# Two gate pieces of mixer B moved into the first 24 blocks of the attention of a hybrid attention layer

## The chip, the cores and the metric

The kernel runs on one core of a Trainium2 chip. The metric is the device time of one execution in microseconds (us). A core has a matrix engine (TensorE, PE in the profile; its weight loads are listed apart as PEld), a vector engine (VectorE, DVE), a scalar engine (ScalarE, ACT), a general engine (GpSimd, POOL), and SyncE (SP), which here only issues DMAs. Each engine works through its own instructions strictly in the order in which the program lists them.

## The reference

One transformer layer works on 128 context tokens ("prompt") and 1024 latent tokens. Cut to what matters here:

```
h = rmsnorm(x, norm_gain) * (1 + scale) + shift
q_a, k_a, v_a, g_a, q_b, k_b, v_b, g_b = split(h @ w_in)
o_a = attention of mixer A (all latent keys and the cached context)
o_b = attention of mixer B (a window of 128, the cached context, a sink)
x + gate * (concat(o_a * silu(g_a), o_b * silu(g_b)) @ w_out)
```

Each mixer has 8 query heads of 64 columns, in 2 groups that share keys and values. The change concerns `g_b`, 512 columns that are computed for all 1152 tokens, and the point at which `w_out` is brought into its working form.

## The kernel before, in words

One pass of PE is not precise enough here, so each 32-bit operand is kept as a high part and a low part, and a product takes three matmuls, high by high, high by low, low by high. `silu(g)` is stored in DRAM (`g_dram`) and read back per unit.

The stages before the attention: the normalised tokens `h` are made and kept in SBUF, high and low, in three thirds of 512, 256 and 384 tokens; then come the gates of A, the queries of A and B, keys and values, and the gates of B. `gates` (L305) walks over thirds and over `ch`, four pieces of 128 columns: one piece is 24 matmuls, 8 steps over k with three products each. That gives 12 pieces for mixer B, the last four 384 tokens wide. Between the matmuls of the last 8 pieces the kernel also runs 24 "max" items and two closings (`beside`, L1050): a score product `pmx` on PE (L881) and its row maximum on DVE (L882), for units 0 and 2.

In the same pieces `w_out` is prepared. It has 16 slabs of 128 by 512. `load_wo` fetches a slab, and `split_wo` (L1032 on) makes its high part with a DVE cast (L1037) and its low part with a subtraction (L1038), on POOL for odd slabs and on DVE for even ones. The parts lie where `h` lay, once that is read for the last time. `WO_STEPS` lists the slabs that are split beside the gates (0 to 10) and `WO_LATE` those split in the attention (11 to 15), each with a block number for its load; its split follows three blocks later.

The attention is a list of units, in the order token tile `t`, group `g`, mixer `m`, the prompt last: 36 units, 0 to 35. A unit of mixer A has nine blocks of keys, one of mixer B three or four. One loop (L1256 on) goes over all blocks, and a "tick" of an agenda starts each. Block `s` issues, in this order: what the agenda holds for this tick, the scores of block `s` (two matmuls `st` into one of two PSUM banks "B", then ACT's exp L1123 and cast L1127, and the low part on POOL L1131; for mixer B four transposes `st` L1115 and a cast L1116), loads of `w_out`, the items that are due (max items for a later unit of A; for a unit of B two matmuls `sn`, a DVE custom operation L942 and ACT's exp L928), up to 2.5 matmuls of the output projection (`po`, L1212) if some are ready, and last the value products of block `s - 3` (`pv`, L1141 to L1144).

A unit of A needs the negated row maxima as extra rows of its query tile: `finish` reduces them, two ticks later PE transposes them (`ptm`, L900), and DVE writes them into `qb` (L901), which the second `st` matmul (L1121) reads. The tick of `finish` is set by `MX_END`: ten blocks after the start of the unit two before.

When the last block of a unit is through, four steps follow at ticks given by `END_AT`: `inverse` (ACT, L1153 or L1155 and L1156), `gated` (two DVE products L1165 that read `pv`, one on POOL), `parts` (high and low output parts `ogh`, `ogl`), and, for a unit of B, the release of 24 output matmuls. `pv` has two banks, so `pv` of a unit waits for `gated` of the unit two before. Output matmuls left at the end run after the loop.

Of the kernel before, what the change touches and what calls it, by code (L numbers as in the profile page):

```python
# [34 lines left out]
KS = (0, 1, 4, 5, 2, 3, 6, 7)  # L35
PL_DVE = (4,)
LAG = 3
LEAD = 4
EARLY = (0, 2)
LOADED = 4  # L40

# [3 lines left out]
MX_AT = (-4, -3, -2, -2, -1, 4, 5, 5, 7, 7, 8, 8)  # L45
MX_FIRST = (0, 1, 2, 2, 3, 4, 4, 5, 6, 6, 7, 8)
PH_DVE = 0
MX_END = 10
SPLIT_LAG = 2

WO_LATE = {12: 8, 13: 9, 11: 21, 14: 22, 15: 23}

WO_STEPS = ((0, 4, 4), (1, 5, 5), (2, 6), (3, 7), (4, 8, 6), (5, 9), (6, 11), (7, 12, 10), (8, 13), (9, 14), (10, 16))
TURN = 2
PUT_LOW = 2
QUERY_AT = (0, 2, 3, 6)
# [52 lines left out]
def hybrid_step(ctx, tc, x_prompt, x_sample, cache_k_a, cache_v_a, cache_k_b, cache_v_b,  # L109
# [800 lines left out]
    def weight_items(i):  # L910
# [93 lines left out]


    wo_raw, wo_parts, wo_big = {}, {}, {}
    STAGE = {0: (1, 0, 7), 1: (0, 0, 7), 2: (1, 0, 6), 3: (0, 0, 6), 4: (1, 0, 7), 5: (0, 0, 7), 6: (1, 0, 7),
             7: (0, 1, 6), 8: (1, 1, 6), 9: (1, 1, 4), 10: (0, 1, 6)}

    def h_slot(lo, i, c, name):  # L1010

# [62 lines left out]
    spare = h_slot(1, 2, 4, "spare").bitcast(F32)  # L1074
    wo_big[2] = h_slot(1, 2, 0, "wo_big2")
    gate = spare[:, 0:512], wo_big[2].bitcast(F32)[:, 1024:1536]
    for n in range(2):
        nc.sync.dma_start(gate[n], gate_row[0:1, 512 * n : 512 * n + 512].to_broadcast([P, 512]))
# [55 lines left out]
    def values(i, b, last, blk, ph, pl):  # L1134
        t, m, g = units[i]
        _, vh, vl = blk
        if b == 0:
            pvb[i] = bank("C", f"pv{i}")
        pv = pvb[i]
        two = vh.rearrange("p s d -> p (s d)")  # L1140
        nc.tensor.matmul(pv, two, ph, start=(b == 0), stop=False)  # L1141
        if m == 0:
            nc.tensor.matmul(pv[0:64, :], vl, ph, start=False, stop=False)  # L1143
        nc.tensor.matmul(pv, two, pl, start=False, stop=last)  # L1144
# [12 lines left out]

        def gated():
            rs = v["rs"]
            o = 768 + 256 * (i % 3)  # L1160
            of = spare[:, o : o + 256].rearrange("p (c n) -> p c n", c=2)
            pvv = pv[0:64, :].rearrange("p (c s n) -> p c s n", s=2, n=P)
            srv = rs.rearrange("p (c s n) -> p c s n", s=2, n=P)
            for s in range(2):
                nc.vector.tensor_tensor(of[64 * s : 64 * s + 64], pvv[:, :, s, :], srv[:, :, s, :],  # L1165
                                        op=ALU.add if m else ALU.mult)
# [32 lines left out]
    def out_items(t, g):  # L1199
# [3 lines left out]
        def mm(n, k, p):  # L1203
# [12 lines left out]
            if k == KS[-1] and p == 2:  # L1216
# [4 lines left out]

        ks = KS[4 * g : 4 * g + 4]
        return [lambda n=n, k=k, p=p: mm(n, k, p)
                for kk in ((ks[:2], ks[2:]) if last else (ks,)) for n in range(2) for k in kk for p in range(3)]

    slots, start = [], []
    for i in range(NU):
# [10 lines left out]
    for i, (t, m, g) in enumerate(units):  # L1238
        if i in EARLY:
            continue  # L1240
        if m == 0:
            items, done = max_items(i)
            at, end = [start[i - 2] + a for a in (MX_AT if i > 2 else MX_FIRST)], start[i - 2] + MX_END
            if t == 0:
                end = start[i] - LEAD
                at = [end - 1]
# [9 lines left out]
            put(s, f)  # L1256
        put(end, done)

    credit, live = 0.0, []
    load_gate(0)  # L1260
    load_gate(1)
    for s in range(len(slots) + LAG + PROMPT_END[3]):
# [83 lines left out]
```

## Time and profile before

| what | value |
| --- | --- |
| median of 3 runs | 711.83 us (711.57 to 713.92) |
| the profiled execution's own time | 711.52 us |
| its span, first to last instruction | 709.6 us |
| PE busy | 691.6 us, 97% |
| DVE, ACT, POOL busy | 469.3, 409.9, 334.2 us |
| last 8 gate pieces of B with max items | 270.5 to 303.1 us |
| blocks 0 to 11 of the attention (units 0 and 1) | 303.18 to 321.90 us |
| blocks 12 to 23 (units 2 and 3) | 321.90 to 341.64 us |
| block 24 | 341.64 to 344.69 us |

A row of the timeline gives the start of an instruction from the span's start, how long it took, engine, line and operation, what it writes and reads, and in brackets the idle time of its engine before it and what ended that. PE's matmuls overlap: a 384-column matmul is listed with 0.34 us, but the next can begin about half of that later, so PE's real pace is the distance between two starts, and PE counts as busy while a gap is shorter than the tail of the matmul before it.

### The profile page before, as it was taken

The page shows a single profiled execution, that of the slowest core. Times are in us where ns is not written, and L with a number is a line of the kernel's source. Part 1 is how long each engine was busy: PE and PEld are TensorE (multiplying, and loading weights), DVE is VectorE, ACT ScalarE, POOL GpSimd, SP SyncE. Part 2 cuts the span into 40 slices and gives each one's busy share as a digit, 9 for nine tenths or more (in the row PEclk, how much of TensorE's full clock was granted, in tenths as well). Part 3 has the DMA queues.
Part 4 walks back from the last instruction along what each step waited for, and adds up shares of the span by engine and source line. Part 5 has one row for each costly group of instructions (what it writes and reads, how often), then busy time and mean ns, then how long its engine had stood idle before and what let it go on. Part 6 is the DMA issues. An engine that isn't in the chain of part 4 may idle for free. (4 is left out here: it accounts for less than half of the span.)

```text
span 709.6 us, 10604 instructions
## 1 busy us (share of the span) xinstructions
PE 691.6 (97%) x3508; PEld 558.5 (79%) x3508; DVE 469.3 (66%) x1019; ACT 409.9 (58%) x829; POOL 334.2 (47%) x356
## 2 busy tenths in 40 slices
PE   7999999999999999989999999999999999999987
PEld 4778988878787889966788888888888888787865
DVE  4667257967848945647867578666775776675662
ACT  5646412412403431188777887787778777877760
POOL 3547023233213421256756655665576557555660
PEclk9999999999999999999999999999999999999999
DMA  8962283358353116332222121212221221222323
GB/s 316 415 211 102 78 302 74 90 154 263 84 139 104 37 39 215 123 108 57 78 68 85 50 82 53 71 57 75 68 82 38 79 71 50 78 72 70 104 67 121
DMA packets 53560, 78.58 MB, mean 111 GB/s; under 512 B 7096, under 2 KB 25720, under 8 KB 52608
## 3 DMA queue, kind: packets, MB, share of 16 engines
q1 hardware_dynamic: 45328, 65.96, 28.1%
q10 hardware_dynamic: 8176, 11.94, 6.3%
q8 instruction: 28, 0.46, 0.3%
q14 instruction: 28, 0.23, 0.1%
HBM read 58.69 MB, written 19.18 MB: 110 GB/s over the span
## 5 line engine op out<-in xcount | busy, mean ns | idle before, releaser
L1131 POOL TENSOR_TENSOR pl<-pe,ph 128x512 fp32r<-128x512 f32 x130 | 167.7, 1292 | 145.0 <-DVE nm L942 67.5
L882 DVE TENSOR_REDUCE mx<-pmx 128x1 f32<-128x384 f32 x192 | 101.4, 552 | 56.3 <-PE pmx L881 54.8
L1123 ACT ACTIVATE pe<-st 128x512 f32<-128x512 f32 x146 | 86.8, 594 | 28.2 <-PE st L1121 27.4
L1127 ACT CAST ph<-pe 128x512 fp32r<-128x512 f32 x146 | 90.6, 621 | 4.8
L1141 PE MATMUL pv<-ph,v_hi 128*128 128x512 f32 x208 | 82.8, 398 | 2.2 <-DVE spare L1165 2.2
L1144 PE MATMUL pv<-pl,v_hi 128*128 128x512 f32 x208 | 82.4, 396 | 0.0
L1212 PE MATMUL po<-wo,ogh 128*128 128x512 f32 x216 | 72.6, 395 | 0.2 <-DVE yt L1219 0.2
L174 POOL TENSOR_TENSOR rs_q<-ms_q,mhalf 128x8 f32<-128x8 f32 x18 | 34.1, 1896 | 80.9 <-DVE ms_q L172 80.9
L942 DVE CUSTOM_DVE_ANT_0 sn<-sn,mask,nsink 128x512 f32<-128x512 f32 (+1 forms) x64 | 46.4, 724 | 38.0 <-PE sn L939 37.6
L881 PE MATMUL pmx<-kha,qt 128*128 128x384 f32 x192 | 61.2, 363 | 0.4 <-ACT pen L928 0.2
L1120 PE MATMUL st<-qt,kha 128*128 128x512 f32 x144 | 58.2, 404 | 1.9 <-ACT pe L1123 1.1
L1121 PE MATMUL st<-qb,kla 68*128 68x512 f32 x144 | 57.5, 399 | 1.1 <-DVE qb L901 1.1
L1143 PE MATMUL pv<-ph,v_lo 128*64 128x512 f32 x146 | 57.6, 395 | 0.0
L1144 PEld LDWEIGHTS pv<-pl,v_hi 128*128 128x128 f32 x208 | 39.2, 189 | 16.4
L928 ACT ACTIVATE pen<-sn,nm 128x512 f32<-128x512 f32 (+2 forms) x72 | 45.0, 626 | 6.5 <-DVE nm L942 3.1
L1116 ACT CAST ph<-st 128x512 fp32r<-128x512 f32 x62 | 36.4, 587 | 19.9 <-PE st L1115 18.7
L1141 PEld LDWEIGHTS pv<-ph,v_hi 128*128 128x128 f32 x208 | 39.3, 189 | 10.6 <-ACT ogh L1177 2.4
L646 ACT CAST qo0q<-ptq 128x512 fp32r<-128x512 f32 x18 | 10.6, 586 | 60.7 <-PE ptq L643 55.8
L1212 PEld LDWEIGHTS po<-wo,ogh 128*128 128x128 f32 x216 | 40.0, 188 | 6.8 <-DVE yt L1219 0.6
L1117 DVE TENSOR_TENSOR pl<-st,ph 128x512 fp32r<-128x512 f32 x62 | 42.5, 686 | 2.7 <-ACT ph L1116 2.1
L1212 PE MATMUL po<-wo,ogl 128*128 128x512 f32 x108 | 42.6, 394 | 0.0
L881 PEld LDWEIGHTS pmx<-kha,qt 128*128 128x128 f32 x192 | 35.6, 191 | 6.4 <-DVE mx L882 1.3
(213 smaller groups left out, 1699.2 us busy)
## 6 DMA issues: line engine op xcount, KB each, us to landing
qt<-qd SPq DMA_DIRECT2D x36, 256.0 KB, 3.0
wm<-in_w_mod_ss_dram SPq DMA_DIRECT2D x7, 1024.0 KB, 10.0
qd<-qo0q ACTq DMA_DIRECT2D x36, 128.0 KB, 2.4
qd<-qo1q ACTq DMA_DIRECT2D x36, 128.0 KB, 2.4
sgl<-gd SPq DMA_DIRECT2D x36, 128.0 KB, 2.2
out_dram<-yt SPq DMA_DIRECT2D x17, 256.0 KB, 2.0
xn<-in_x_sample_dram SPq DMA_DIRECT2D x8, 512.0 KB, 7.2
wg<-in_w_mod_g_dram SPq DMA_DIRECT2D x4, 1024.0 KB, 8.3
```

What stands on the lines that cost most here:

```text
L881: nc.tensor.matmul(pm[:, 0:384], lhs, kha[:, g, 3 * b : 3 * b + 3, :], start=True, stop=True)
L882: nc.vector.tensor_reduce(mx[:, h, b : b + 1], pm[:, 0:384], axis=AX.X, op=ALU.max)
L942: nc.vector.tensor_tensor_reduce(s, s, mask[:, m0 : m0 + n], -1.0, nsink[:, 4 * g + h : 4 * g + h + 1], op0=ALU.add, op1=ALU.min, accum_ou ...
L1120: nc.tensor.matmul(s, kh, qtile[i], start=True, stop=False)
L1121: nc.tensor.matmul(s, kl, qbtile[i], start=False, stop=True)
L1123: nc.scalar.activation(pe, s, AF.Exp)
L1127: nc.scalar.copy(ph, pe)
L1131: nc.gpsimd.tensor_tensor(pl, pe, ph, op=ALU.subtract)
L1141: nc.tensor.matmul(pv, two, ph, start=(b == 0), stop=False)
L1143: nc.tensor.matmul(pv[0:64, :], vl, ph, start=False, stop=False)
L1144: nc.tensor.matmul(pv, two, pl, start=False, stop=last)
L1212: nc.tensor.matmul(po[n], a, wo_parts[KT * n + k][lo], start=(k == KS[0] and p == 0), stop=(k == KS[-1] and p == 2))
```

## The change

The last two pieces of B's gates (`ch` 2 and 3, the third of 384 tokens) are no longer computed in the gate stage: `gb` runs six pieces after the first four instead of eight, and the max items stand closer (over 48 steps of k and not 64). ACT copies the 256 columns of weights that the two pieces need, high and low, into the places of `h`'s second third (`keep`, 16 copies); these are the places in which slabs 8 to 11 of `w_out` are later put. The 48 matmuls (`late_product`) go into a queue of which each block takes two (`LATE_RATE`), just ahead of its value products; they fill PSUM banks "D" and "E", which the output projection takes over afterwards. `silu` of a finished piece is then built from ACT's Exp and three DVE operations on 384 columns, add, reciprocal and product, since the attention's function table on ACT holds no Silu. The result tile is one of the three buffers `pe` of the attention's exponentials. Slabs 7, 8, 9 and 10 of `w_out` are split in the attention and no longer beside the gates, and 11 to 15 later than before.

Three smaller edits: the maxima of a unit of A are closed three blocks before the unit starts (`MX_LEAD`; for a unit behind a three-block unit of B, which are units 4 and 30, this is one block earlier than before, for the others the same), with `LEAD` one larger for the prompt's units; units 31 and on of the latent tokens (that is, unit 31) take their last steps at ticks 1, 2, 3, 5 and not 1, 4, 6, 9 (`END_LAST`); and the prompt's first 24 output matmuls run one half of the columns after the other.

The diff, cut to its core:

```diff
-LEAD = 4
+LEAD = 5
...
-MX_END = 10
+MX_LEAD = 3
...
-WO_LATE = {12: 8, 13: 9, 11: 21, 14: 22, 15: 23}
+WO_LATE = {8: 22, 9: 23, 12: 25, 13: 26, 7: 28, 10: 29, 11: 32, 14: 33, 15: 35}
...
+LATE_RATE = 2
...
+END_LAST = (1, 2, 3, 5)
+ENDING = 31
...
-    beside[:2] = 0.0, (len(beside[2]) + 0.5) / 64
+    beside[:2] = 0.0, (len(beside[2]) + 0.5) / 48
...
-    for n, _ in enumerate(gb):
-        if n == 4:
-            for i in (7, 8, 9):
-                load_wo(i)
+    kept = {}
+    def keep(k):
+        for lo, src in enumerate((W_GB.hi[k], W_GB.lo[k])):
+            if k % 2 == 0:
+                kept[lo, k // 2] = h_slot(lo, 1, k, f"kept{lo}_{k}")
+            o = 256 * (k % 2)
+            nc.scalar.copy(kept[lo, k // 2][:, o : o + 256], src[:, 256:512])
+    for n in range(6):
+        next(gb)
+        if n == 3:
+            for k in range(KT):
+                later(1 + k // 2, lambda k=k: keep(k))
...
+    def late_product(ch, w, x, k, first, last):
+        if first:
+            pgl[ch] = bank("DE"[ch % 2], f"pgl{ch}")[:, 0:384]
+        o = 256 * (k % 2) + P * (ch - 2)
+        nc.tensor.matmul(pgl[ch], kept[w, k // 2][:, o : o + P], h_at(x, 2, k, slice(0, 384)), start=first, stop=last)
+        if last:
+            later(1, lambda: late_gate(ch))
+
+    def late_gate(ch):
+        sg = w3.tile([P, 512], F32, tag="pe", name=f"sgl{ch}", bufs=PES)[:, 0:384]
+        nc.scalar.activation(sg, pgl[ch], AF.Exp, scale=-1.0)
+
+        def quotient():
+            nc.vector.tensor_scalar(sg, sg, 1.0, None, op0=ALU.add)
+            nc.vector.reciprocal(sg, sg)
+            nc.vector.tensor_tensor(sg, pgl[ch], sg, op=ALU.mult)
+            nc.sync.dma_start(g_dram[512 + P * ch : 512 + P * ch + P, 768:TOK], sg)
+
+        later(1, quotient)
...
-        ends = END_AT if t else PROMPT_END
+        ends = (END_LAST if i >= ENDING else END_AT) if t else PROMPT_END
...
-            at, end = [start[i - 2] + a for a in (MX_AT if i > 2 else MX_FIRST)], start[i - 2] + MX_END
+            at, end = [start[i - 2] + a for a in (MX_AT if i > 2 else MX_FIRST)], start[i] - MX_LEAD
...
+        late += LATE_RATE
+        while lateq and late >= 1.0:
+            lateq.pop(0)()
+            late -= 1.0
```

How the program's order moves, at three places. First PE in block 5 of the attention. In the names, `st0_5` are the scores of unit 0, block 5, and `pv0` the value sums of unit 0. Before:

```order
L1120 MATMUL st0_5_3458<-qt0_2962,kha_2318 128x512
L1121 MATMUL st0_5_3458<-qb0_3154,kla_2319 128x512
L1141 MATMUL pv0_3440<-ph0_2_3412,v_hi_2324 128x512
L1143 MATMUL pv0_3440<-ph0_2_3412,v_lo_2325 64x512
L1144 MATMUL pv0_3440<-pl0_2_3413,v_hi_2324 128x512
L1120 MATMUL st0_6_3472<-qt0_2962,kha_2318 128x512
```

Now, with `pgl2` and `pgl3` as the sums of the two moved pieces:

```order
L1164 MATMUL st0_5_3410<-qt0_2962,kha_2318 128x512
L1165 MATMUL st0_5_3410<-qb0_3116,kla_2319 128x512
L1102 MATMUL pgl2_3336<-h1_2_0_141,kept0_0_3183 128x384
L1102 MATMUL pgl3_3338<-h1_2_0_141,kept0_0_3183 128x384
L1185 MATMUL pv0_3390<-ph0_2_3358,v_hi_2324 128x512
L1187 MATMUL pv0_3390<-ph0_2_3358,v_lo_2325 64x512
L1188 MATMUL pv0_3390<-pl0_2_3359,v_hi_2324 128x512
L1164 MATMUL st0_6_3426<-qt0_2962,kha_2318 128x512
```

Two products have come in between the scores and the values. Second, DVE around blocks 25 and 26, where `sn5_1` and `sn5_2` are scores of unit 5 (mixer B) and `wraw` the slabs of `w_out`. Before:

```order
L1037 CAST wo_big0_3553<-wraw14_3795 128x512
L1038 TENSOR_TENSOR wo_big2_3362<-wraw14_3795,wo_big0_3553 128x512
L942 ISA sn5_1_3880,nm5_3852<-sn5_1_3880,mask_2959,nsink_105 128x512
L942 ISA nm5_3852 128x1
L1037 CAST wo_big1_3554<-wraw15_3820 128x512
L942 ISA sn5_2_3900,nm5_3852<-sn5_2_3900,mask_2959,nsink_105 128x512
```

And now the same stretch:

```order
L1039 CAST wo0_8_3852<-wraw8_3783 128x512
L1040 TENSOR_TENSOR wo1_8_3853<-wraw8_3783,wo0_8_3852 128x512
L945 ISA sn5_1_3870,nm5_3835<-sn5_1_3870,mask_2959,nsink_105 128x512
L945 ISA nm5_3835 128x1
L1039 CAST wo0_9_3878<-wraw9_3808 128x512
L1111 TENSOR_SCALAR sgl3_3857<-sgl3_3857 128x384
L1112 RECIPROCAL sgl3_3857<-sgl3_3857 128x384
L1113 TENSOR_TENSOR sgl3_3857<-pgl3_3338,sgl3_3857 128x384
L945 ISA sn5_2_3898,nm5_3835<-sn5_2_3898,mask_2959,nsink_105 128x512
```

Slabs 8 and 9 stand where 14 and 15 stood (those follow later, after 12, 13, 7, 10 and 11), and the second piece's three operations stand ahead of `sn5_2`. Third, PE at the end of the loop, where `pv34` and `pv35` are the value sums of the prompt's last two units and `po8_0` is the output of the last latent tile. Before:

```order
L1144 MATMUL pv34_8035<-pl34_0_7988,v_hi_2324 128x512
L1141 MATMUL pv35_8057<-ph35_0_8017,v_hi_2324 128x512
L1144 MATMUL pv35_8057<-pl35_0_8018,v_hi_2324 128x512
L1212 MATMUL po8_0_7886<-wo0_2_3088,ogh30_7998 128x512
L1212 MATMUL po8_0_7886<-wo1_2_3089,ogh30_7998 128x512
```

Now:

```order
L1188 MATMUL pv34_8071<-pl34_0_8021,v_hi_2324 128x512
L1256 MATMUL po8_0_7919<-wo0_2_3097,ogh30_8031 128x512
L1256 MATMUL po8_0_7919<-wo1_2_3098,ogh30_8031 128x512
L1256 MATMUL po8_0_7919<-wo0_2_3097,ogl30_8032 128x512
L1256 MATMUL po8_0_7919<-wo0_3_3122,ogh30_8031 128x512
L1256 MATMUL po8_0_7919<-wo1_3_3123,ogh30_8031 128x512
L1256 MATMUL po8_0_7919<-wo0_3_3122,ogl30_8032 128x512
L1185 MATMUL pv35_8097<-ph35_0_8053,v_hi_2324 128x512
L1188 MATMUL pv35_8097<-pl35_0_8054,v_hi_2324 128x512
```

Six output products of the last latent tile now stand between `pv34` and `pv35`.

More of the change, by code (lines that the diff above doesn't have):

```diff
@@ L47 @@
 PH_DVE = 0
-MX_END = 10
+MX_LEAD = 3
 SPLIT_LAG = 2
-WO_LATE = {12: 8, 13: 9, 11: 21, 14: 22, 15: 23}
-WO_STEPS = ((0, 4, 4), (1, 5, 5), (2, 6), (3, 7), (4, 8, 6), (5, 9), (6, 11), (7, 12, 10), (8, 13), (9, 14), (10, 16))
+WO_LATE = {8: 22, 9: 23, 12: 25, 13: 26, 7: 28, 10: 29, 11: 32, 14: 33, 15: 35}
+WO_STEPS = ((0, 4, 4), (1, 5, 5), (2, 6), (3, 7), (4, 8, 6), (5, 9), (6, 11))
+LATE_RATE = 2
 TURN = 2
@@ L1006, in hybrid_step @@
     wo_raw, wo_parts, wo_big = {}, {}, {}
-    STAGE = {0: (1, 0, 7), 1: (0, 0, 7), 2: (1, 0, 6), 3: (0, 0, 6), 4: (1, 0, 7), 5: (0, 0, 7), 6: (1, 0, 7),
-             7: (0, 1, 6), 8: (1, 1, 6), 9: (1, 1, 4), 10: (0, 1, 6)}
+    STAGE = {0: (1, 0, 7), 1: (0, 0, 7), 2: (1, 0, 6), 3: (0, 0, 6), 4: (1, 0, 7), 5: (0, 0, 7), 6: (1, 0, 7)}
     def h_slot(lo, i, c, name):
@@ L1073, in hybrid_step, with open_spare @@
     w3 = ctx.enter_context(tc.tile_pool(name="w3", bufs=4, side="right"))
[L1074 to L1078, printed above, removed]
+    spare, gate = None, None
+    def open_spare():
+        nonlocal spare, gate
+        spare = h_slot(1, 2, 4, "spare").bitcast(F32)
+        wo_big[2] = h_slot(1, 2, 0, "wo_big2")
+        gate = spare[:, 0:512], wo_big[2].bitcast(F32)[:, 1024:1536]
+        for n in range(2):
+            nc.sync.dma_start(gate[n], gate_row[0:1, 512 * n : 512 * n + 512].to_broadcast([P, 512]))
+    pgl = {}
+    def late_product(ch, w, x, k, first, last):
[14 more added lines that the diff above has]
+        later(1, quotient)
+    lateq = [(ch, 0, 1, k, k == 4, False) for k in (4, 5, 6, 7, 0, 1, 2, 3) for ch in (2, 3)]
+    for ch in (2, 3):
+        lateq += [(ch, w, 0, k, False, w == 1 and k == KT - 1) for k in range(KT) for w in range(2)]
+    lateq = [lambda a=a: late_product(*a) for a in lateq]
+    lateq.insert(16, open_spare)
     ogp = ctx.enter_context(tc.tile_pool(name="ogp", bufs=NOG, side="right"))
@@ L1223, in out_items @@
         return [lambda n=n, k=k, p=p: mm(n, k, p)
-                for kk in ((ks[:2], ks[2:]) if last else (ks,)) for n in range(2) for k in kk for p in range(3)]
+                for kk in ((ks[:2], ks[2:]) if last and g else (ks,)) for n in range(2) for k in kk for p in range(3)]
     slots, start = [], []
@@ L1257, in hybrid_step @@
         put(end, done)
-    credit, live = 0.0, []
+    credit, live, late = 0.0, [], 0.0
     load_gate(0)
```

## The prediction

> **What bounds the kernel now.** I read the page first. PE is busy for nearly the whole span:
>
> ```profile
> span 709.6 us, 10604 instructions
> PE 691.6 (97%) x3508; PEld 558.5 (79%) x3508; DVE 469.3 (66%) x1019; ACT 409.9 (58%) x829; POOL 334.2 (47%) x356
> ```
>
> Then windows of 20 us show where PE is not (columns: length, then busy time and instructions of PE, PEld, DVE, ACT, POOL, the clock, DMA):
>
> ```profile
> 280.00:300.00 20.00, 20.00 (x127) 19.91 (x127) 14.59 (x29) 2.24 (x5) 5.17 (x4) 1.00 0.39 125
> 300.00:320.00 20.00, 17.96 (x88) 13.41 (x87) 9.35 (x22) 15.48 (x32) 10.45 (x10) 1.00 0.35 105
> 320.00:340.00 20.00, 18.38 (x86) 13.38 (x84) 14.43 (x34) 17.04 (x36) 14.89 (x16) 1.00 0.21 61
> 340.00:360.00 20.00, 19.36 (x87) 15.24 (x85) 14.55 (x30) 16.11 (x33) 14.42 (x16) 1.00 0.26 75
> 400.00:420.00 20.00, 20.00 (x100) 16.09 (x99) 13.61 (x29) 15.20 (x31) 11.20 (x12) 1.00 0.22 65
> ```
>
> The gate stage (first row) and the settled attention (last row) are full; the first 25 blocks of the attention, from 303 to 345 us, are not. Idle time understates it, since a PE gap shows only beyond the tail of the matmul before. So I count starts. PE's timeline at the end of the gates, in block 3, and at four transposes:
>
> ```profile
> 301.56 0.33 PE L263 MATMUL pg<-h,whigb 128*128 128x384 f32 x1
> ...
> 302.95 0.34 PE L259 MATMUL pg<-h,whigb 128*128 128x384 f32 x1
> ...
> 308.76 0.44 PE L938 MATMUL sn<-khb,qt 128*128 128x384 f32 x1 [0.49 <-ACT pen L928]
> ...
> 309.44 0.40 PE L1143 MATMUL pv<-ph,v_lo 128*64 128x512 f32 x1
> 309.68 0.39 PE L1144 MATMUL pv<-pl,v_hi 128*128 128x512 f32 x1
> 309.91 0.39 PE L1120 MATMUL st<-qt,kha 128*128 128x512 f32 x1
> ...
> 316.50 0.60 PE L1115 MATMUL st<-ident_r,pen 128*128 128x128 f32 x4
> 316.85 0.42 PE L881 MATMUL pmx<-kha,qt 128*128 128x384 f32 x1
> ```
>
> From 301.56 to 302.95 lie eight steps: 0.174 us for a 384-column matmul. A 512-column one takes 0.235 / 0.233, four transposes 0.35 us. Blocks 0 to 11 hold 45 matmuls of 512 (18 `st` and 27 `pv` of unit 0's nine blocks), 13 of 384 (8 `sn`, 5 `pmx`) and 12 transposes: 10.5 + 2.3 + 1.05 = 13.8 us of work. Blocks 12 to 23 hold 53 of 512 (18 `st`, 33 `pv`, 2 `po`), 20 of 384 (8 `sn`, 12 `pmx`) and 12 transposes: 12.3 + 3.5 + 1.05, with two small ones 17.0 us. Against that stands what they took:
>
> ```profile
> 303.18:321.90 18.72, 15.86 (x74) 10.90 (x72) 8.74 (x20) 16.83 (x35) 10.45 (x10) 1.00 0.34 98
> 321.90:341.64 19.74, 18.94 (x87) 13.93 (x88) 14.21 (x34) 16.28 (x35) 15.19 (x16) 1.00 0.26 78
> 344.69:367.10 22.41, 22.41 (x110) 18.00 (x109) 15.98 (x33) 17.11 (x35) 15.25 (x16) 1.00 0.29 85
> ```
>
> So 4.9 us of PE are free in blocks 0 to 11 and 2.7 in 12 to 23. What holds PE there is ACT, first of all; its timeline in blocks 1 and 7:
>
> ```profile
> 305.18 0.60 ACT L1123 ACTIVATE pe<-st 128x512 f32<-128x512 f32 x1
> 305.81 0.62 ACT L1127 CAST ph<-pe 128x512 fp32r<-128x512 f32 x1
> 306.33 0.57 ACT L928 ACTIVATE pen<-sn,nm 128x384 f32<-128x384 f32 x1
> 306.81 0.19 ACT L928 ACTIVATION_READ_ACCUMULATOR pen<-sn,nm 128x1 f32 x1
> 306.90 0.58 ACT L1123 ACTIVATE pe<-st 128x512 f32<-128x512 f32 x1
> ...
> 315.56 0.59 ACT L1123 ACTIVATE pe<-st 128x512 f32<-128x512 f32 x1
> ...
> 316.71 0.59 ACT L1123 ACTIVATE pe<-st 128x512 f32<-128x512 f32 x1
> ```
>
> A block with an item of unit 1 costs ACT 306.90 - 305.18 = 1.72 us, a block without one 1.15 us. PE needs 0.81 us in blocks 0 to 2 (two `st`, two `sn`), 1.51 in block 3 and 1.16 in blocks 4 to 7.
>
> **The change, term by term**, against the profiled execution's 711.52 us (span 709.6 and 1.9 around it; 0.3 below the median of 711.83).
>
> 1. Gate stage. 48 matmuls of 0.174 us leave a stretch in which PE has no gap: -8.35 us. The max items of two units now share six pieces with the splits of slabs 0 to 6. DVE's 14.6 us of 20 rise to about nine tenths, so PE may wait now and then for a bank: 0 to 1.3 us, taken 0.2, since the row has room left. ACT's 16 copies of 128x256 lie in a stage where it is busy 2.2 us of 20, on time.
>
> 2. Blocks 0 to 11 get 24 matmuls, 4.2 us. In blocks 0 to 3 ACT stays the bound (1.72 against 0.81 + 0.35, in block 3 1.51 + 0.35), and the products are free but for the last pair, which stands behind block 3's wait (the row of 308.76): +0.35. From block 4 on PE needs 1.51 us against ACT's 1.15 and becomes the bound: five blocks give +1.1 over today's pace (0.35 each, less 0.6 of gaps). In 9 to 11 the two products fill today's gaps, among them one behind slabs 12 and 13, whose splits leave. Together +1.45 (0.7 to 2.6).
>
> 3. Blocks 12 to 23: 17.0 + 4.2 = 21.2 us of work against 19.74 taken today: +1.4 if every gap closes. Gaps inside a block's max items stand ahead of the products and don't close: I leave 1.0 us. +2.4 (1.4 to 4.2, where no gap closes).
>
> 4. Unit 4's `qb`, one block earlier, and unit 30's, likewise. PE waits for both:
>
> ```profile
> 342.73 0.50 PE L1121 MATMUL st<-qb,kla 68*128 68x512 f32 x1 [0.64 <-DVE qb L901]
> 343.07 0.40 PE L938 MATMUL sn<-khb,qt 128*128 128x512 f32 x1
> ...
> 651.47 0.50 PE L1121 MATMUL st<-qb,kla 68*128 68x512 f32 x1 [0.49 <-DVE qb L901]
> ```
>
> To the idle time come the tail of the matmul before (0.16, which is 0.39 less 0.23) and a slow restart (343.07 - 342.73 = 0.34 for 0.24): 0.9 and 0.75 us. Block 24 also takes the last product, 0.17. -0.7 and -0.8 (0 to -0.9 each); nothing is late next in block 25, since the row of 344.69 us on shows PE full.
>
> 5. The two results take a `pe` buffer each, from Exp until their store has landed, and the third exponential after them waits for that. Behind it in ACT stand the casts that POOL and the value products need, but these have three blocks of lead, about 5 us at 19.74 us for twelve. 0 to 3 us, taken 0.4.
>
> 6. DVE in blocks 25 to 38. Here the change moves work to where POOL runs beside it. Four groups, the slabs split beside the gates (`wo`) and those split in the attention (`wo_big`), and one such case on POOL and DVE:
>
> ```profile
> L1037 DVE CAST wo<-wraw 128x512 fp32r<-128x512 f32 x12 | 5.7, 476 | 0.0
> L1038 DVE TENSOR_TENSOR wo<-wraw,wo 128x512 fp32r<-128x512 f32 x6 | 4.2, 693 | 0.3
> L1037 DVE CAST wo_big<-wraw 128x512 fp32r<-128x512 f32 x4 | 2.4, 597 | 0.0
> L1038 DVE TENSOR_TENSOR wo_big<-wraw,wo_big 128x512 fp32r<-128x512 f32 x2 | 2.4, 1178 | 0.1
> ...
> 344.65 1.33 POOL L1131 TENSOR_TENSOR pl<-pe,ph 128x512 fp32r<-128x512 f32 x1 [1.34 <-ACT ph L1127]
> 344.87 1.67 DVE L1038 TENSOR_TENSOR wo_big<-wraw,wo_big 128x512 fp32r<-128x512 f32 x1
> ```
>
> The subtraction of 344.87 ends 0.56 us after POOL's operation, as if it had only begun then. From 344.69 to 367.10 us DVE is busy 15.98 of 22.41. It loses slabs 14 and 15 as timed today (about 2.8) and gains eight casts and four subtractions: by the `wo` rows 6.6 us, by the `wo_big` rows 9.5 us. The second gate's three operations add about 1.8 (0.6 each, from 0.69 for 512 columns). DVE then has 21.6 to 24.5 us of work in 22.41. PE may run about two blocks ahead of DVE's `sn` and `mx` before it stands, some 2 us, so I take 1.0 us of waiting (0 to 4).
>
> [...]
>
> 7. The end. Two waits of `pv` for a bank:
>
> ```profile
> 682.20 0.39 PE L1212 MATMUL po<-wo_big,ogh 128*128 128x512 f32 x1
> 683.53 0.47 PE L1141 MATMUL pv<-ph,v_hi 128*128 128x512 f32 x1 [0.94 <-DVE spare L1165]
> ...
> 687.32 0.47 PE L1141 MATMUL pv<-ph,v_hi 128*128 128x512 f32 x1 [0.69 <-DVE spare L1165]
> ```
>
> The first starts 1.33 us after a 0.23 us matmul, so 1.1 is lost; it waits for unit 31's `gated`, which `END_LAST` puts two ticks earlier. Before the second, six output products (1.4 us) are put, more than its 0.69 and the drain. -1.1 and -0.9: -2.0 (-0.5 to -2.2). All else there is a queue of ready output products, so the end moves with it.
>
> Sum: -8.35 + 0.2 + 1.45 + 2.4 - 0.7 - 0.8 + 0.4 + 1.0 - 2.0 = -6.4 us. From the median, 711.8 - 6.4 = 705.4. All terms at their good ends (0, 0.7, 1.4, -0.9 twice, 0, 0, -2.2) give -10.3, or 701.5.
>
> **The rivals.**
>
> A. The gaps don't close: what ends them is latency between engines (bank, exponential, cast), and each product delays the next score and so the chain. Then the 8.35 us come back in full, and terms 4 and 7 alone stay: 711.8 - 3.5 + 1.4 for terms 5 and 6 = 709.7, the edge of no change. For it: idle pieces are short, 0.2 to 0.9 us. Against it: in blocks 0 to 3 ACT runs without a break. Chance 0.11.
>
> B. Slower: DVE becomes the bound in blocks 25 to 38. If each moved cast and subtraction and the second gate's operations wait for a whole POOL operation, DVE has 13.2 + 8 x (0.42 + 1.33) + 4 x (0.61 + 1.33) + 1.8 = 36.8 us of work in 22.41: 14.4 over, less 2 of slack, in place of term 6's 1.0: 705.4 + 11.4 = 716.8. From 7.4 us of waiting on the change loses. Against it: the `wo_big` casts lose 0.12 us on average, not 1.33, and POOL is busy two thirds of the time. Chance 0.05.
>
> C. The reciprocal is slow. [...] Plain, in the first row; against it, the two below on DVE's smallest operations:
>
> ```profile
> L882 DVE TENSOR_REDUCE mx<-pmx 128x1 f32<-128x384 f32 x192 | 101.4, 552 | 56.3 <-PE pmx L881 54.8
> ...
> L977 DVE RECIPROCAL inv<-sum 128x4 f32<-128x4 f32 x18 | 3.0, 168 | 1.1 <-POOL sum L974 1.1
> L172 DVE TENSOR_SCALAR ms_k<-ssk 128x4 f32<-128x4 f32 x9 | 1.5, 170 | 0.3
> ```
>
> Four columns cost no more than in a plain operation. Chance 0.09. [...]
>
> **How the numbers follow.** The forecast, gaps close for the most part and DVE keeps up, has 0.75, with a range of its own of 702 to 708. A, B and C have 0.11, 0.05 and 0.09. The range 702.0 to 709.4 takes in C and most of the bad ends of terms 2, 3 and 6, and leaves out B and half of A. A measurement of this kernel can tell 0.3%, 2.1 us, from no change: faster means below 709.7. That holds for the forecast, C, and part of A: 0.88; the same 0.07; slower 0.05.
>
> **What would show it.** The gate stage ends about 8 us earlier (about 295). Blocks 0 to 24 take some 44.5 us, not 41.5; over 48 says A. [...] In blocks 25 to 38 PE shows at most 1 to 2 us of idle time behind DVE; much more, with DVE full, says B. The waits for `qb` and the two for L1165 at the end are gone. If PE's idle time falls as told and the time doesn't, my count of its work is wrong.

## The result and the profile after

The changed kernel takes 719.25 us (median of 6 runs, 718.07 to 721.81) against 711.71 for the kernel before (6 runs): 1.0104 times as long, 95% interval 1.0091 to 1.0118. It is slower by 7.5 us, where 6.4 less were forecast. The profiled execution took 719.1 us, with a span of 717.3.

The page's first lines, as in the prediction. PE is busy for 1.7 us more and DVE for 9.1, in a span that is 7.7 us longer:

```profile
span 717.3 us, 10629 instructions
PE 693.3 (97%) x3508; PEld 560.7 (78%) x3508; DVE 478.4 (67%) x1025; ACT 414.5 (58%) x845; POOL 336.8 (47%) x356
```

Busy time by stage, of the changed kernel (columns as before: length, busy time of PE, PEld, DVE, ACT, POOL, clock, DMA). A stage begins at the first `st` of its first block: blocks 0 to 11, 12 to 23, 24, 25 to 36, 37 to 49. Under it, the last of these stages in the kernel before:

```profile
296.76:316.52 19.76, 18.99 (x96) 15.41 (x96) 8.40 (x19) 16.39 (x33) 10.51 (x10) 1.00 0.22 66
316.52:345.01 28.49, 25.39 (x113) 20.48 (x111) 17.62 (x36) 17.63 (x37) 14.01 (x15) 0.88 0.21 64
345.01:347.27 2.26, 2.26 (x12) 1.87 (x10) 1.64 (x5) 1.92 (x4) 0.00 (x0) 1.00 0.13 37
347.27:374.68 27.41, 23.28 (x110) 17.89 (x109) 24.88 (x44) 18.15 (x37) 20.09 (x19) 1.00 0.36 113
374.68:399.58 24.90, 24.12 (x116) 19.13 (x116) 17.93 (x39) 18.61 (x37) 15.74 (x16) 1.00 0.27 84
```

```profile
367.10:390.96 23.86, 23.86 (x116) 19.24 (x116) 17.70 (x38) 18.74 (x38) 14.09 (x15) 1.00 0.22 66
```

The second row is the one to look at: 28.49 us where 22.1 were forecast, and the only row whose clock is not 1.00. The fourth shows DVE busy 24.88 of 27.41 us. Set against the kernel before, with the forecast of the same stretch (E1 and E11 are experiments, told below):

| stretch, us | before | forecast change | after: change | E1: change | E11: change |
| --- | --- | --- | --- | --- | --- |
| start of the attention | 303.18 | -8.15 | -6.42 | -7.11 | -6.75 |
| blocks 0 to 11 | 18.72 | +1.45 | +1.04 | +1.02 | +1.02 |
| blocks 12 to 23 | 19.74 | +2.4 | +8.75 | +2.94 | +3.45 |
| block 24 | 3.05 | -0.7 | -0.79 | -0.80 | -0.79 |
| blocks 25 to 49 | 46.27 | +1.0 | +6.04 | +4.59 | +1.49 |
| from block 50 to the end of the span | 318.64 | -2.8 | -0.92 | +0.66 | -1.52 |
| span | 709.6 | -6.4 (with +0.4 for the buffers) | +7.7 | +1.3 | -3.1 |

What PE waited for and for how long in total, how often, and the longest time, in the changed kernel (the rows on stages before the gates are left out):

```profile
PE pmx L884 <- DVE mx L885: 3.4, 3, 2.9
...
PE st L1159 <- DVE pen L983: 2.0, 3, 1.3
PE pv L1185 <- DVE spare L1209: 1.7, 1, 1.7
PE st L1164 <- DVE pl L1161: 1.3, 1, 1.3
```

The two waits for `qb` (L904 now) ahead of `st` are gone, as told. What stands in their place is DVE's in the main; one wait of 0.8 us in block 42 is for ACT's exponential. The groups of the three DVE operations on 384 columns, which the prediction took at 0.6 us each (busy time in total, mean ns of one):

```profile
L1112 DVE RECIPROCAL sgl<-sgl 128x384 f32<-128x384 f32 x2 | 5.1, 2554 | 0.1
L1111 DVE TENSOR_SCALAR sgl<-sgl 128x384 f32<-128x384 f32 x2 | 1.3, 630 | 0.0
L1113 DVE TENSOR_TENSOR sgl<-pgl,sgl 128x384 f32<-128x384 f32 x2 | 1.1, 557 | 0.1
```

The reciprocal takes four times the mean of either plain operation. (The two adds took 0.91 us, the row below, and 0.35.) DVE and PE around the first reciprocal, in blocks 19 and 20 (timeline: start, duration, idle time before and its releaser), and the clock after it:

```profile
329.42 0.91 DVE L1111 TENSOR_SCALAR sgl<-sgl 128x384 f32<-128x384 f32 x1
330.36 2.55 DVE L1112 RECIPROCAL sgl<-sgl 128x384 f32<-128x384 f32 x1
332.95 0.56 DVE L1113 TENSOR_TENSOR sgl<-pgl,sgl 128x384 f32<-128x384 f32 x1
333.42 1.01 DVE L885 TENSOR_REDUCE mx<-pmx 128x1 f32<-128x384 f32 x2
```

```profile
329.12 0.51 PE L884 MATMUL pmx<-kha,qt 128*128 128x384 f32 x2
...
330.74 0.39 PE L1165 MATMUL st<-qb,kla 68*128 68x512 f32 x1
334.02 1.15 PE L884 MATMUL pmx<-kha,qt 128*128 128x384 f32 x2 [2.89 <-DVE mx L885]
...
336.49 0.63 PE L1185 MATMUL pv<-ph,v_hi 128*128 128x512 f32 x1
336.92 0.63 PE L1187 MATMUL pv<-ph,v_lo 128*64 128x512 f32 x1
```

```profile
334.03:340.86 6.83, 6.64 (x18) 4.96 (x19) 3.45 (x9) 0.82 (x2) 2.13 (x3) 0.50 0.36 108
```

Block 20 has three max items. The two of block 19 (329.12) hold both banks for them, and their maxima stand behind the reciprocal; so the first of block 20 finds no bank, and PE stands for 2.89 us. After it a 512-column matmul starts every 0.43 us (336.49, 336.92) and not every 0.23: the granted clock is 0.50 from 334.03 to 340.86 us, so PE runs at half pace for 6.83 us. Blocks 20 and 21 lose 5.2 and 1.6 us to this pair, wait and half pace, against what their matmuls need.

**The theory I took to the chip (T1):** the reciprocal's length in DVE's queue makes PE stand, and the standing makes PE slow; together some 8 us. **The rivals:** the load that the late slabs of `w_out` put on DVE is what costs, and the reciprocal is a detail (T2); the products have no room in blocks 12 to 23 (T3).

### The profile page after: what moved, and what is told of

It reads as the page before. It is cut to its first block, busy times and chain, and to the rows that moved or that the text cites. A ratio compares the mean times of both kernels' runs of the same rounds, so it can differ in the third digit from the quotient of the medians.

```text
span 717.3 us, 10629 instructions
## 1 busy us (share of the span) xinstructions
PE 693.3 (97%) x3508; PEld 560.7 (78%) x3508; DVE 478.4 (67%) x1025; ACT 414.5 (58%) x845; POOL 336.8 (47%) x356
## 4 chain that ended last, share of the span: by engine, by line
PE 85%; DVE 7%; ACT 2%; DMA 2%; issue 1%; POOL 1%; ACTq 0%; SPq 0%; POOLq 0%; DVEq 0%
PE po L1256 13%; PE pv L1185 6%; PE pv L1188 6%; PE pq L254 5%; PE pq L252 5%; PE pq L253 5%; PE pmx L884 4%; PE pv L1187 4%; PE st L1164 4%; PE st L1165 4%; PE st L1159 4%; PE pg L262 3%; PE pg L266 3%; PE pg L267 3%; PE sn L941 2%; PE sn L942 2%
```

## The experiments

Each kernel was timed beside the kernel before; the ratio is to that, with its 95% interval. Between two kernels of this list I compare ratios, since the median of the kernel before moves by 0.9 us from series to series.

**E1. The quotient on ACT.**

```
-            nc.vector.tensor_scalar(sg, sg, 1.0, None, op0=ALU.add)
-            nc.vector.reciprocal(sg, sg)
+            nc.scalar.activation(sg, sg, AF.Ln, bias=1.0)
+            nc.scalar.activation(sg, sg, AF.Exp, scale=-1.0)
```

> The changed kernel with the two late gates' 1/(1+e) taken by ACT (Ln of 1+e, then Exp of its negative, 384 columns each) in place of DVE's add and reciprocal; DVE keeps the product alone. T1 (the 2.55 us reciprocal holds DVE's queue, PE stands 2.9 us behind it, and TensorE then runs at half pace for some 6 us; the second costs 2 us): the window 320 to 340 us shows a clock near 1.00 again, the row of 2.89 us for mx is gone, and the time falls by 3 + 3 + 2 us, to about 711. T2 (the reciprocal is a detail; DVE's load by the slabs split after block 22 costs the time): at most 3 us less, 716 or more. T3 (the products themselves find no room in blocks 12 to 23): blocks 12 to 23 stay above 26 us, and 717 or more.

Measured: 713.09 us, 1.0028 (1.001 to 1.0046), so 0.76% less than the changed kernel. The window from 320 to 340 us, in which blocks 15 to 24 lie, is whole again:

```profile
320.00:340.00 20.00, 19.77 (x99) 15.83 (x98) 14.05 (x30) 15.82 (x35) 12.65 (x14) 1.00 0.24 77
```

Blocks 12 to 23 take 22.68 us, 2.94 more than before the change, where the prediction had 2.4; blocks 0 to 24 take 44.67 against its "some 44.5". T3 falls. T2 falls as far as it calls the reciprocal a detail. But 1.3 us of span above the kernel before remain where the forecast had 6.4 below, and for that the rest of the table speaks: blocks 25 to 49, and the end.

**E2. The same reciprocal in three parts of 128 columns, over three ticks.**

```
-            nc.vector.reciprocal(sg, sg)
+            third(0)
+            later(1, lambda: third(1))
+            later(2, product)
...
+        def third(n):
+            nc.vector.reciprocal(sg[:, P * n : P * n + P], sg[:, P * n : P * n + P])
```

> The changed kernel with each late reciprocal cut into three of 128 columns, one per tick, so that DVE's work is the same to a tenth of a microsecond and only the length of one piece changes (2.55 to about 0.85 us each). T1 (length in DVE's queue, not load): PE's waits behind DVE in blocks 20, 21 and 27 fall under 1 us each, no drop of the clock, time about 711 to 713. T2 (DVE's load): as the changed kernel, 717 to 719.

Measured: 720.13 us, 1.011 (1.0088 to 1.0133), the same as the changed kernel. PE's waits, the reciprocal's group, and DVE around the first one:

```profile
PE pmx L884 <- DVE mx L885: 2.9, 2, 1.5
PE po L1264 <- DVE sgl L1121: 2.7, 1, 2.7
```

```profile
L1117 DVE RECIPROCAL sgl<-sgl 128x128 f32<-128x128 f32 x6 | 5.6, 940 | 0.1
```

```profile
329.81 1.76 DVE L1117 RECIPROCAL sgl<-sgl 128x128 f32<-128x128 f32 x2
331.49 0.95 DVE L885 TENSOR_REDUCE mx<-pmx 128x1 f32<-128x384 f32 x2
332.36 0.94 DVE L1117 RECIPROCAL sgl<-sgl 128x128 f32<-128x128 f32 x1
```

In block 20 the same 2.9 us stand, now in two waits of 1.44 and 1.48 us. The cut didn't spread the parts: two ran back to back and the third stands 0.8 us later, all among the maxima of blocks 19 and 20. T1 as I had put it, the length of one piece, is not borne out, though 1.76 us stayed in one piece and E2 alone doesn't part length from amount. The sum of the waits, which didn't change, speaks for the amount of DVE's work in that stretch (T2's kind of cause, but in a place of two blocks), and so do E3 and E5 below; E1 gained by taking the work off DVE. The second quotient brought a wait of its own making: its bank stays taken two ticks longer, and the output projection waits 2.7 us for it.

**E3. E1 with the late slabs earlier.**

```
-WO_LATE = {8: 22, 9: 23, 12: 25, 13: 26, 7: 28, 10: 29, 11: 32, 14: 33, 15: 35}
+WO_LATE = {7: 8, 8: 16, 9: 18, 12: 22, 13: 23, 10: 25, 11: 27, 14: 28, 15: 30}
```

> The kernel of the ACT quotient, and besides all nine late slabs of w_out split earlier: 7 at block 8, 8 at 16, 9 at 18, 12 and 13 at 22 and 23, 10, 11, 14, 15 at 25 to 30, so none later than block 30. T1 (the late slabs in blocks 33 to 38, with SyncE held 6.6 us by the two loads of yt, cost the rest): PE's waits for pl and ptm and the split's wait for its load in those blocks go, and about 4 us less than the kernel of the ACT quotient alone, near 707. T2 (any split in the attention that runs beside POOL costs the same wherever it stands): within 1 us of it, since the waits move to blocks 8 to 30.

Measured: 714.17 us, 1.0037 (1.0023 to 1.005), not distinguishable from E1. Blocks 25 to 49 take 49.14 us against 50.86, but block 20 now holds the split of slab 9 and waits 1.82 us:

```profile
334.61 0.90 PE L884 MATMUL pmx<-kha,qt 128*128 128x384 f32 x2 [1.82 <-DVE mx L885]
```

The waits moved, as the rival said; the expected 4 us didn't come. Here it is another piece of DVE's work that makes PE stand in block 20.

**E4. The small edits alone, on the kernel before** (`LEAD`, `MX_LEAD`, `END_LAST`, the output parts split in the last half only).

> The kernel before with the small edits alone: LEAD 5, MX_LEAD, END_LAST for unit 31 and the output parts split only in the last half. The prediction's terms 4 and 7: -0.7 - 0.8 - 2.0 = -3.5 us, to 708.2. The reading of the changed kernel's trace: the two waits for qb go (-1.5), the tail gains nothing since unit 31's gated in front of the last max part takes the time that its earlier end frees, so about -1.5, to 710.2, with a wait of st for pen at the end.

Measured: 711.76 us, 0.999 (0.9976 to 1.0004): no change that can be told. Block 24 falls from 3.05 to 2.16 us, and the block of the wait for unit 30's `qb` from 2.80 to 2.07, so 1.6 us are gained. The end gives them back: PE waits there three times for `pen`, 2.3 us in all and 1.6 at the longest, and half pace follows (E7 below).

**E5. The reciprocal on 256 of 384 columns.**

```
-            nc.vector.reciprocal(sg, sg)
+            nc.vector.reciprocal(sg[:, 0:256], sg[:, 0:256])
```

> The changed kernel with the two late reciprocals on 256 of their 384 columns; the last 128 columns of both pieces keep 1+e in place of 1/(1+e). At 6.6 ns a column each takes 1.7 us in place of 2.55. If PE's wait is simply the reciprocal's length (no slack in block 20), the wait for mx falls from 2.9 to about 2.0 us; in the kernel of earlier slabs a wait of 1.8 us, and in the changed kernel one of 1.74, were followed by full pace. T1 (half pace follows only idle times above some 2 to 2.5 us): no slow stretch, so 0.9 + 0.9 of waiting and 3 to 3.7 of pace go: 714.5 to 715.5. Rival (half pace follows any wait of this kind, or comes from something else in this stretch): only 1.7 us go, 717.5.

Measured: 718.65 us, 1.0083 (1.005 to 1.0116), with single runs from 713.45 to 722.36. The wait fell as told, to 2.1 us, and half pace followed all the same; it also followed a wait of 2.0 us for `pl` in block 36. The reciprocal's group, the longest waits, and the two windows:

```profile
L1112 DVE RECIPROCAL sgl<-sgl 128x256 f32<-128x256 f32 x2 | 3.5, 1753 | 0.1
```

```profile
PE pmx L884 <- DVE mx L885: 2.8, 3, 2.1
...
PE st L1164 <- DVE pl L1161: 2.0, 1, 2.0
```

```profile
320.00:340.00 20.00, 17.71 (x71) 13.98 (x70) 12.41 (x27) 13.29 (x30) 13.62 (x15) 0.83 0.16 44
...
360.00:380.00 20.00, 16.84 (x77) 12.90 (x76) 16.13 (x31) 10.36 (x19) 12.41 (x12) 0.91 0.26 81
```

Waits of 2.1 and 2.0 us were enough here, and the 3.19 us of E10 below were not, so the threshold of 2 to 2.5 us that I had guessed isn't there. PE's wait fell by 0.8 us with a reciprocal 0.8 us shorter, so in block 20 DVE's time is PE's. The spread tells more than the median: the run of 713.45 us had a mean granted clock of 0.999, those of 716.6 to 720.2 had 0.992 or 0.993, that of 722.36 had 0.985. As an estimate, 717 us times 0.7% is 5.0 us: the same program takes about 713.5 or about 718.5, as the clock falls or not.

**E6. E1 with the casts of all nine late slabs on ACT.**

```
-        nc.vector.tensor_copy(hi, raw)
+        if i < 7:
+            nc.vector.tensor_copy(hi, raw)
+        else:
+            nc.scalar.copy(hi, raw)
```

> The kernel of the ACT quotient with the casts of the nine late slabs moved from DVE to ACT; the subtractions stay. ACT is busy 13.55 of 20 us there, DVE waits up to 1.25 us in a cast for its slab to land. If what PE waits for in blocks 25 to 42 (5.4 us lost there, 1.2 before the change) is DVE held by these casts, the waits for pmx, ptm and pl in blocks 33 to 36 go and the time falls by 2.5 to 4, to 709 to 710.5. If the landing itself is late (SyncE held by yt), ACT waits in its place, with exponentials and casts behind it: no gain, 712.5 to 714.

Measured: 713.43 us, 1.0015 (1.0001 to 1.0029), against E1 a tenth of a per cent less, inside both intervals. Blocks 33 to 36 take 7.81 us where E1 took 9.71, but blocks 27 and 29 take 2.4 us more, with waits for ACT's exponential and for the maxima. Neither reading holds alone.

**E7 and E8. `END_LAST` undone**, in E1 and in E4:

```
-        ends = (END_LAST if i >= ENDING else END_AT) if t else PROMPT_END
+        ends = END_AT if t else PROMPT_END
```

> The kernel of the ACT quotient with unit 31 back at END_AT in place of END_LAST, all else kept. The prediction's term 7 (the earlier gated frees PE's bank: -1.1): this kernel then loses 1.1, 714.2. The reading of the traces (the earlier gated stands ahead of the last max parts on DVE and PE waits 2.0 us for pen, before the change 1.1 for the bank): 0.6 to 2 us less than with END_LAST, 711 to 712.5, the row st <- pen gone and pv <- spare back.

> The kernel before with LEAD 5, MX_LEAD and the output parts split only in the last half, without END_LAST. Both readings give the two waits for qb (-0.9 and -0.75); the six output products before the last bank give up to -0.9 more if term 7's second half holds. Against the kernel of all small edits (711.76): lower by 1 to 2 if END_LAST is what cost there. Expected 709.8 to 710.5, 1.5 to 2.2 below before; if END_LAST cost nothing, 711.8.

Measured: E7 711.42 us, 0.9989 (0.9977 to 1.0001), where E1 had 1.0028: 0.39% less, 2.8 us. E8 710.12 us, 0.9966 (0.9953 to 0.9978), where E4 had 0.999: 0.24% less, 1.7 us, and faster than the kernel before. So `END_LAST` costs, on both grounds. But not in the way that the expectation of E7 names (`gated` ahead of the max parts on DVE). DVE and POOL at the end of E1, then of E7:

```profile
682.66 0.18 DVE L980 RECIPROCAL inv<-sum 128x4 f32<-128x4 f32 x1 [1.08 <-POOL sum L977]
682.88 2.61 DVE L983 TENSOR_SCALAR pen<-pen,inv 128x128 f32<-128x128 f32 x4
```

```profile
681.73 0.74 POOL L1211 TENSOR_TENSOR spare<-spare,sgl 128x256 f32<-128x256 f32 x1 [1.50 <-DVE spare L1209]
682.43 0.20 POOL L977 TENSOR_TENSOR sum<-sum,ex 128x4 f32<-128x4 f32 x1
682.58 1.26 POOL L1175 TENSOR_TENSOR pl<-pe,ph 128x512 fp32r<-128x512 f32 x1
683.81 1.40 POOL L1223 TENSOR_TENSOR ogl<-spare,ogh 128x256 fp32r<-128x256 f32 x2
```

```profile
682.23 0.88 DVE L983 TENSOR_SCALAR pen<-pen,inv 128x128 f32<-128x128 f32 x4
```

The earlier `gated` has a product on POOL (L1211), which now stands ahead of the sum that unit 35's `inv` needs, and the operations that POOL does after it fall beside DVE's four `pen`: 2.61 us where E7 has 0.88. PE waits for them three times, 1.32, 0.35 and 0.36 us. In E1's profile half pace follows; in the changed kernel, with the same three waits (1.32, 0.35, 0.35), it doesn't, and the clock stands at 1.00 in the same place (694.08 to 697.50 us). E1:

```profile
686.13:689.55 3.42, 3.42 (x9) 2.57 (x9) 1.63 (x4) 1.85 (x4) 2.10 (x3) 0.50 0.14 41
```

From block 50 to the end of the span it is 319.3 us in E1, 317.7 in the changed kernel and 317.1 in E7. So in these profiles `END_LAST` costs 0.6 us without half pace behind it and 2.2 with it.

**E9. Useless work in the wait.** The changed kernel, with

```
+            if ch == 2:
+                later(2, fill)
...
+        def fill():
+            for _ in range(14):
+                nc.tensor.matmul(pgl[3], kept[0, 3][:, 0:128], h_at(0, 2, 7, slice(0, 384)), start=False, stop=False)
```

> The changed kernel with 14 useless products of 384 columns (14 x 0.175 = 2.45 us of TensorE) put ahead of block 20's scores, where PE waits 2.89 us behind the first reciprocal; they add into the second piece's sum, so that piece's values are others. Nothing is taken from DVE. T1 with the clock as a cost of its own (the wait of 2.9 us costs 2.9 and then about 3.7 more, because the clock falls to half after it): the wait shrinks to 0.5, the clock stays at 1.00, the useless work costs nothing and the time falls by 2.5 to 4, to 715.5 to 717. Rival (half pace has to do with DVE or memory in this stretch, not with PE standing idle): no gain, 719, or up to 2.5 more.

Measured: 717.47 us, 1.006 (1.004 to 1.0079), where the changed kernel has 1.0104 (1.0091 to 1.0118): 2.45 us more matmuls, and 0.44% less time, 3.1 us. Block 20:

```profile
329.69 2.62 PE L1120 MATMUL pgl<-h,kept 128*128 128x384 f32 x14
...
333.22 0.90 PE L884 MATMUL pmx<-kha,qt 128*128 128x384 f32 x2 [0.44 <-DVE mx L885]
334.31 0.44 PE L884 MATMUL pmx<-kha,qt 128*128 128x384 f32 x1 [0.19 <-DVE mx L885]
```

```profile
320.00:340.00 20.00, 19.32 (x99) 15.80 (x99) 15.03 (x28) 13.15 (x30) 12.77 (x14) 1.00 0.17 56
```

DVE's operations are the same, the waits are 0.44 and 0.19 us, and the clock stays at 1.00 in this window. Half pace is thus a price of PE's standing, and one of its own: what the first reciprocal takes from PE in the changed kernel is the wait and then as much again (half of 6.83 us is 3.4).

**E10 and E11. The pieces that helped, together:** the ACT quotient, `END_AT`, casts of slabs 7, 10, 11, 14 and 15 on ACT, and in E11 also

```
+WO_LATE = {7: 12, 8: 22, 9: 23, 12: 25, 13: 26, 10: 28, 14: 29, 11: 33, 15: 34}
```

> The changed kernel with the ACT quotient, unit 31 back at END_AT, and the casts of slabs 7, 10, 11, 14 and 15 on ACT, while those of 8, 9, 12 and 13 stay on DVE: in the kernel with all nine on ACT the waits of blocks 33 to 36 fell from 3.5 to 1.7 us and new ones of 2.3 us came in blocks 27 and 29, where 12 and 13 stand. If each wait goes with the queue that its cast stands in, this kernel keeps the gain without the new waits: 1.5 to 2 under the kernel of the ACT quotient with END_AT (711.42), about 709.5, 0.3% under the kernel before. If the sum of waits stays the same whichever engine casts: 711.4.

> As the one before, with other places for the late slabs: 7 at block 12 (its place is free by then), 10 and 14 one block further from the heavy maxima at 28 and 29, 11 and 15 at 33 and 34. If the remaining waits in blocks 33 to 42 hang on the moment of each split, the sum of waits in blocks 25 to 49 falls below 2 us and the time to 708.5 to 709.5; if on the amount, as the one before within 0.5 us.

Measured: E10 711.81 us, 0.9993 (0.9978 to 1.0008), as E7; the 709.5 expected of it didn't come. E11 708.23 us, **0.9936 (0.9923 to 0.9949)**, 0.64% less than the kernel before and the fastest here. What E10 lost is one wait in block 36, shown by ACT's and DVE's timeline:

```profile
361.57 0.62 ACT L1040 CAST wo<-wraw 128x512 fp32r<-128x512 f32 x1 [1.06 <-DMA wraw<-in_w_out_dram]
...
364.75 0.62 ACT L1040 CAST wo_big<-wraw 128x512 fp32r<-128x512 f32 x1 [2.08 <-DMA wraw<-in_w_out_dram]
```

```profile
365.40 0.69 DVE L1043 TENSOR_TENSOR wo_big<-wraw,wo_big 128x512 fp32r<-128x512 f32 x1 [3.02 <-ACT wo_big L1040]
```

Slabs 11 and 14 haven't landed when the cast's turn comes: the raw slabs share two buffers, and a load is issued only when POOL's or DVE's subtraction has given one back. ACT stands, DVE stands behind ACT, and PE waits 3.19 us for the low part `pl` behind both, with no half pace after it. In the changed kernel the same wait was DVE's own:

```profile
369.76 0.43 DVE L1039 CAST wo<-wraw 128x512 fp32r<-128x512 f32 x1 [1.25 <-DMA wraw<-in_w_out_dram]
```

In E11 no cast waits for its slab, and blocks 37 to 49 take 23.83 us, as before the change (23.84).

**E12. E7 with E11's places for the slabs, all casts on DVE.**

> The kernel of the ACT quotient with END_AT (711.42) and the slabs' new places alone (7 at block 12, 10 and 14 at 28 and 29, 11 and 15 at 33 and 34), all nine casts on DVE. If the waits of blocks 33 to 42 come from the moment of slab 11's load (its buffer is given back by POOL's subtraction of slab 7, and the split stands in DVE's queue before the slab has landed), this kernel is as fast as the one that also has casts on ACT (708.23): 708 to 709.2, no row of a cast waiting for its slab. If the amount of DVE's work there is what costs, it keeps most of the loss: 710.5 to 711.5.

Measured: 709.90 us, 0.9967 (0.9955 to 0.998): between E7 (0.9989) and E11 (0.9936). Blocks 25 to 49 take 49.36 us, against 50.53 in E7 and 47.76 in E11. Of the 2.8 us that separate those two, 1.2 go with the moment of the splits and 1.6 with the engine of the casts, that is DVE's load, which leaves a wait of 1.43 us for the maxima in block 33, behind a cast of 1.41 and a subtraction of 1.64 us. Each reading holds for about a half.

## Why the prediction was wrong, step by step

The range 702.0 to 709.4 missed, on the other side. The span shows 7.7 us more where the steps summed to 6.4 less, and of the 14.1 us between them steps 3 (6.35) and 6 (5.0) hold most. For step 1, PE's last gap ahead of the key and gate matmuls before the change, then the same and the one wait among the gates of B after it:

```profile
228.72 0.63 PE L745 MATMUL ptk<-ident_r,k2k 128*128 128x128 f32 x4 [1.25 <-DVE klp L763]
```

```profile
228.91 0.63 PE L748 MATMUL ptk<-ident_r,k2k 128*128 128x128 f32 x4 [1.24 <-DVE klp L766]
...
286.12 0.44 PE L884 MATMUL pmx<-kha,qt 128*128 128x384 f32 x1 [0.87 <-DVE qb L904]
```

For step 6, DVE's subtractions in the changed kernel:

```profile
L1040 DVE TENSOR_TENSOR wo<-wraw,wo 128x512 fp32r<-128x512 f32 x6 | 5.1, 856 | 0.2
...
L1040 DVE TENSOR_TENSOR wo_big<-wraw,wo_big 128x512 fp32r<-128x512 f32 x2 | 1.4, 692 | 0.1
```

- **Step 1, the gate stage (-8.15).** The 48 matmuls did go, and the attention starts 6.4 us earlier, in E1 7.1. But from the gap at 228.7 us to the attention PE takes 67.85 us where it took 74.46, 6.6 less and not 8.35, and it is 67.8 in every run with the moved pieces. So the closer max items cost 1.7 us, outside the 0 to 1.3 given: 1.1 is the wait for `qb` with its restart, the rest steps that grew by 0.1 to 0.2 beside the two closings. Only the other 0.2 (in E1 0.5 the other way) lies ahead of this stage and differs from run to run.
- **Steps 2 and 3, the products in blocks 0 to 23.** Right as a mechanism: +1.02 and +2.94 in E1, for +1.45 and +2.4, where 4.2 us of matmuls were added to each. Most of the gap time of blocks 0 to 11 and about half of that of blocks 12 to 23 took them in, so rival A, by which all 8.35 us come back, is out. The changed kernel's own blocks 0 to 24 take 50.51 us, over the 48 that was to say A; E1's 44.67 shows that this sign was ambiguous, since C raises the same number.
- **Step 3 in the changed kernel: +8.75.** This is rival C, with 0.09. The step that failed is the price of the quotient on DVE. Step 3 counts nothing for the first piece's three operations, and step 6 prices the second's at "(0.6 each, from 0.69 for 512 columns)", where the reciprocal measured 2.55: that priced a reciprocal by another function's row, and the one reciprocal in the trace of before, of four columns (168 ns), is too short to show a cost per column. C had the cause, but the price behind its place in the range, a multiple of a plain operation, no run shows; the rows show 2.55 us for 384 columns, against means of 0.63 for the add and 0.56 for the product. Nor has block 20, with three max items, the "some 2 us" of step 6 before PE stands, and no step counts the half pace after a wait (a clock of 0.50 for 6.83 us). Against E1, which also takes the add off DVE, the first reciprocal costs 5.8 us (14.50 against 8.70 in blocks 20 to 23) and the second, in block 27, 1.4.
- **Step 4, `qb`.** Right: -0.79 and -0.73.
- **Step 5, the `pe` buffers (+0.4).** Nothing of it shows: in E1, which takes the same buffers, PE loses nothing in blocks 18 and 19 and 0.1 us each in 21 to 23, no more than before.
- **Step 6, DVE in blocks 25 to 38 (+1.0, 0 to 4).** Mis-sized: +6.0 in blocks 25 to 49, of which the reciprocal is 1.4. "PE may run about two blocks ahead" didn't hold where a split, or a cast whose slab hasn't landed, meets DVE's maxima; the buffers of the raw slabs were not in the sum at all. E11, with the quotient and five casts on ACT and other places, brings the +6.0 to +1.5. Rival B, splits made longer by POOL, doesn't show in the sum: DVE's eight subtractions take 6.5 us before and after (`wo` 693 and then 856 ns on average, `wo_big` 1178 and then 692). What changed is the place in which they stand. Why blocks 27 and 33 still lose 1.5 us in E11 was not tried.
- **Step 7, the end (-2.0).** Failed: -0.2 without step 4's wait. The `pv` waits went, and 2.0 us of waits for `pen` came in their place (E7). I had looked at DVE's part of `gated` alone, although its POOL part is one of the instructions that move.

Of the 7.5 us by which the medians differ, the clock is nearly half, as an estimate that takes PE for the bound wherever the clock was low: the changed kernel's runs had a median granted clock of 0.992, which is 5.7 us of its span, those of the kernel before (27 runs beside E1) 0.997, or 2.1 us. The profile agrees: half of the 6.83 us in blocks 20 and 21 is 3.4.

Even E11 has only half of what was forecast: its span is 3.1 us below the kernel before, not 6.4.

Left open: which waits are followed by half pace. In the attention of the profiles here, those of 2.89, 2.69 (E2), 2.1 and 2.0 us were, and two of 1.44 and 1.48 us close together; those of 1.74, 1.82, 1.92 (E9, block 36) and 3.19 us weren't. The three waits for `pen` at the end were in E1 (0.50 from 686.13 to 689.55 us) and E4 (0.66 from 685 to 690 us), and weren't in the changed kernel, E2, E3, E5 and E6 (1.00). In E8 half pace (308.73 to 312.14 us; the clock is 0.91 over 300 to 320 us) followed waits of 0.80, 0.48 and 0.48 us in blocks 2 and 3, which the profile of the kernel before shows too, with the clock at 1.00. So the length of the wait doesn't decide it.

## What to carry to other kernels

Price an operation from a row of its own function at a size where the columns show, or keep its whole range in the forecast; a tiny row doesn't tell it (here four columns took 168 ns and 384 took 2554). Slack belongs to a place, not to a kernel: before anything is put into an in-order queue, look at what that queue has to do in those two blocks, whether its data have landed, and which other queues the same step stands in. And count a stall of the matrix engine with the half pace that may follow: here that added 3.4 us after a wait of 2.89 us and 1.7 after three of 1.32, 0.35 and 0.36 us, and nothing after one of 3.19 us.

## What the runs showed of the hardware

- DVE's reciprocal in 32-bit takes 940 ns for 128 columns, 1753 for 256 and 2554 for 384: 6.3 ns a column and 0.13 us beside; the two plain adds of 384 columns took 350 and 910. With Ln and Exp on ACT (E1) PE stands for 0.23 us in all from 320 to 340 us.
- After PE has stood it may go on at half pace: in the changed kernel, after a wait of 2.89 us, 512-column matmuls start every 0.43 us and not every 0.23, at a granted clock of 0.50 for 6.83 us; in E1, after waits of 1.32, 0.35 and 0.36 us, the clock is 0.50 for 3.42 us. With useless matmuls in place of the wait (E9, 0.44 and 0.19 us left) it stays at 1.00. The same waits were followed by half pace in one run and not in another: `pen` in E1 (0.50) and in the changed kernel (1.00). E5's runs, with mean clocks from 0.985 to 0.999, point the same way. That 2.1 and 2.0 us were enough (E5: 0.83 and 0.91 over 20 us), and 3.19 once were not (E10: 1.00 from 360 to 380 us), says that no length decides alone; what decides was not shown.
- The four `pen` scalings of 128x128 take 0.22 us each with POOL idle (E7) and 0.65 beside POOL's operations (E1): 0.88 and 2.61 for four.
- ACT loads a function table between the last Silu of the gates and the attention's first exponential: 1.28 us at 303.88 us before the change and at 297.28 in the changed kernel. Either trace has one more load, of the same length, ahead of the first Silu, and the attention's Exp and Ln bring none.
